# The gate rows and the angle tables of a mixed mLSTM and attention block, given out in 36 small steps

## The chip, the core and the metric

The kernel runs on one core of one Trainium2 chip. Five engines run side by side, each with its own queue of instructions: TensorE (PE) multiplies matrices and transposes, VectorE (DVE), ScalarE (ACT) and GpSimd (POOL) work on elements, and SyncE (SP) starts most of the DMA transfers. PE writes its results to PSUM, which has eight banks here, each of 128 partitions by 512 fp32. The metric is the device time of one execution in microseconds (us), the median over several runs.

## The reference, cut to what matters

One layer is computed for 1024 positions of 1024 numbers, in fp32. A normalized input is projected to twelve segments; two branches follow (an mLSTM over four heads, and differential attention over eight heads), and they are mixed.

```python
proj = jnp.einsum('bsd,de->bse', h, w_in[layer])
(a_q, a_k, a_v, a_o, a_z, a_g, b_q, b_k, b_v, b_z, g_a, g_b) = jnp.split(proj, _split_points(), axis=-1)
qk = jax.nn.silu(centred_depthwise_conv(jnp.concatenate([a_q, a_k], axis=-1), ml_conv_w[layer]))
gates = (a_g.reshape(B, S, 4, ML_HEADS) + ml_gate_b[layer]).transpose(2, 0, 3, 1)
i_fw, lf_fw = gates[0], jax.nn.log_sigmoid(gates[1])
i_bw, lf_bw = gates[2], jax.nn.log_sigmoid(gates[3])
# mlstm: b = cumsum(f); running maximum of i - b; m_t, weights exp(...) and decay per chunk
y_a = hm * jax.nn.sigmoid(a_o) * jax.nn.silu(a_z)
ang = positions[..., None] * inv_freq          # rope: cos(ang), sin(ang) turn b_q and b_k
```

The change touches where the small work is done that depends on `a_g` alone (log-sigmoid, cumulative sums, running maxima, the maximum carried from chunk to chunk, the weights) and on `positions` alone (angles, sines, cosines, two tables). It computes the same numbers.

## The kernel before

**Stages.** The projections come first, then the attention, then the mLSTM, then the mixing. This document is about the second part of the projections, the *pairs' stage*. Numbers are kept as two parts (H and L), so one logical product takes three matmuls.

**Pairs.** `self.pairs` has 16 entries, numbered 0 to 15. Each projects two blocks of 128 columns at once by Strassen's scheme (`pair_units`): seven products, f0 to f6 here, of twelve 128x512 matmuls each (L279), in 14 units of six matmuls. A product writes one PSUM bank under the tag `T`. Its bank is read by ACT (f0, L285), by DVE (f1, f2, f3, L282), and by a *sink* (f3 to f6). I write 8.f3 for product f3 of pair 8.

- Even pairs project columns of `ak` or `aq` and end in `conv_sink`: L344 adds the product to what is saved and writes `cin`, then a convolution with five taps is run in four parts (ACT L358, four times DVE L360, ACT L361, DVE L363, ACT L366, POOL L369). Each part takes a bank `T` of its own. I call these four banks A, B, C and D in their order; each becomes free with its L363.
- Odd pairs project columns of `ao` and `az` and end in `oz_sink` (DVE L318 and L319, ACT L321 and L326), which takes no further bank.

**Weights.** The seven weight forms of a pair are rounded on ACT (L256), and their low parts are made on POOL or DVE (L258), some four products ahead.

**Banks.** Six banks have the tag `T` in this stage (`banks("ps0", T=6)`). A product or a transpose that wants one waits until the last reader of the bank's former content is done.

**The small work.** `ml_gates` returns the products of the gate columns (L667, L668) and three functions. `rows` brings the gates through DRAM into rows of 64 partitions and makes the log-sigmoid, cumulative sums and running maxima; its tiles are named `gch`. `chain` transposes the ends of the chunks (PE L131), carries the maximum over the chunks and `weights` transposes it back and makes four rows of weights. `columns` turns these by nine transposes into columns (`gc_...`, `dec128`). `angle_loads` and `angles` load the positions, transpose them once, reduce the angle (tile `wk`), take sine and cosine on ACT (tile `an`) and copy them to two wide tiles (`rep`). `tables` turns each `rep` by eight transposes, in two banks, into `cosT` and `sinT`, which the next stage reads. `an`, `wk`, both `rep`, and the sinks' `cin`, `y` and `oz` share six buffers of the tag `big`.

**What sets the order.** In this stage PE alone keeps the order in which the program is written (`keep(E.PE)`). DVE, ACT, POOL and SP are put in order by a scheduler, which goes by the written order and by when it believes the operands to be ready. Every engine then works strictly in its order. The written order of the small work is:

```python
more = {1: gl + gmm, 4: [chain], 5: [weights], 6: [columns], 7: [do(self.angle_loads)], 8: [do(self.angles)],
        10: tab[0:2], 11: tab[2:4]}
for i in range(len(self.pairs)):
    w.add(*more.get(i, []), *self.pair_units(i, sinks[i]))
```

So each piece stands as a whole ahead of a pair; `rows` is called with the last gate product, ahead of pair 1.

Of the kernel before, what the change touches and what calls it, by code (L numbers as in the profile page):

```python
# [14 lines left out]
S = 1024  # L15
# [94 lines left out]
class Block:  # L110
# [473 lines left out]
    def angle_loads(self):  # L584
# [6 lines left out]
        posf, self.scol = an[0:8, 672:800], an[:, 808:809]  # L591
# [4 lines left out]
    def angles(self):  # L596


        v, a, an = self.v, self.a, self.an
# [7 lines left out]
        sn, cs = t3(an, 0), t3(an, 1)  # L607
        v.tensor_tensor(out=ang, in0=pos.unsqueeze(2).broadcast_to([128, 8, 32]),
                        in1=self.inv.unsqueeze(1).broadcast_to([128, 8, 32]), op=ALU.mult)
        v.tensor_scalar(out=u, in0=ang, scalar1=1.0 / (2.0 * PI), scalar2=None, op0=ALU.mult)  # L610
        magic = 1.5 * 2.0 ** 23
        v.tensor_scalar(out=nh, in0=u, scalar1=magic * 4096.0, scalar2=None, op0=ALU.add)
        v.tensor_scalar(out=nh, in0=nh, scalar1=-magic * 4096.0, scalar2=None, op0=ALU.add)
        v.tensor_tensor(out=u, in0=u, in1=nh, op=ALU.subtract)
        v.tensor_scalar(out=nl, in0=u, scalar1=magic, scalar2=None, op0=ALU.add)
        v.tensor_scalar(out=nl, in0=nl, scalar1=-magic, scalar2=None, op0=ALU.add)
        for part in two_pi_parts():
            for n in (nh, nl):
                v.scalar_tensor_tensor(out=ang, in0=n, scalar=-part, in1=ang, op0=ALU.mult, op1=ALU.add)
        lim = float(np.nextafter(np.float32(PI), np.float32(0)))  # L620
        v.tensor_scalar(out=ang, in0=ang, scalar1=lim, scalar2=-lim, op0=ALU.min, op1=ALU.max)
        v.tensor_scalar(out=u, in0=ang, scalar1=-1.0, scalar2=None, op0=ALU.mult)
        v.tensor_tensor(out=u, in0=u, in1=ang, op=ALU.max)
# [3 lines left out]
        self.reps = []  # L627
        for src in (cs, sn):
            rep = self.big("rep")[:, 0:S].rearrange("p (k a b) -> p k a b", k=8, a=4)
            v.tensor_copy(rep, src.unsqueeze(2).broadcast_to([128, 8, 4, 32]))  # L630
            self.reps.append(rep)

    def tables(self, i, g):

        if g == 0:
            n = ("cosT", "sinT")[i]
            setattr(self, n, self.tab.tile([128, S], F32, name=n, tag=n))
        dst = getattr(self, ("cosT", "sinT")[i])
        ps = self.bank("T")
        for k in range(4):  # L640
            self.tr(ps[:, k * 128:(k + 1) * 128], self.reps[i][:, 4 * g + k].rearrange("p a b -> p (a b)"))
        self.v.tensor_scalar(out=dst[:, g * 512:(g + 1) * 512], in0=ps, scalar1=self.scol[:, 0:1], scalar2=None, op0=ALU.mult)


    def ml_gates(self):
# [15 lines left out]
        def products(half, part):  # L661
# [9 lines left out]
            if part == 1:  # L671
# [4 lines left out]
                if half == 1:  # L676
                    rows()

        def rows():
            gd = X["gd"]  # L680
# [7 lines left out]
            p.memset(one, 1.0)  # L688
            v.tensor_scalar(out=nx, in0=x, scalar1=-1.0, scalar2=None, op0=ALU.mult)
            v.tensor_tensor(out=nx, in0=nx, in1=x, op=ALU.min)  # L690
            a.activation(out=e, in_=nx, func=AF.Exp)
            v.tensor_scalar(out=u, in0=e, scalar1=1.0, scalar2=None, op0=ALU.add)
# [3 lines left out]
            a.activation(out=iu, in_=ln, func=AF.Exp, scale=-1.0)  # L696
            v.tensor_tensor(out=u, in0=u, in1=iu, op=ALU.mult)
# [4 lines left out]
            for d in range(2):  # L702
                r = slice(32 * d, 32 * d + 32)
                st = slice(None) if d == 0 else slice(None, None, -1)
                v.tensor_tensor_scan(out=b[r, st], data0=one[r, st], data1=lf[r, st], initial=0.0, op0=ALU.mult, op1=ALU.add)
            v.tensor_tensor(out=g, in0=ig, in1=b, op=ALU.subtract)
            for d in range(2):
                r = slice(32 * d, 32 * d + 32)
                st = slice(None) if d == 0 else slice(None, None, -1)
                v.tensor_tensor_scan(out=cm[r, st], data0=g[r, st], data1=g[r, st], initial=-3.0e38, op0=ALU.max, op1=ALU.max)  # L710
            gg = self.dram.tile([2, 4 * NC, L], F32, name="gg")
# [4 lines left out]
            for d in range(2):  # L716
# [3 lines left out]
                v.tensor_copy(ends[r, 1:2], cm[r, c:c + 1])  # L720

        def chain():
# [10 lines left out]
            for i in range(NC - 1):  # L733
                for d in range(2):
                    c, n = (i, i + 1) if d == 0 else (NC - 1 - i, NC - 2 - i)
                    v.tensor_tensor(out=vw(mr, d, n), in0=vw(mr, d, c), in1=vw(er[:, 64:128], d, c), op=ALU.max)
                    v.tensor_tensor(out=vw(mr, d, n), in0=vw(mr, d, n), in1=vw(er[:, 0:64], d, c), op=ALU.add)

        def weights():
# [6 lines left out]
            M, sint, emt, ws, nml, dec = one, u, iu, ln, small(1), small(1)  # L746
            v.tensor_scalar(out=M, in0=cm, scalar1=mst[:, 0:1], scalar2=None, op0=ALU.max)
            a.activation(out=sint, in_=M, func=AF.Exp, scale=-1.0, bias=mst[:, 0:1])
            v.tensor_scalar(out=sint, in0=sint, scalar1=0.5, scalar2=None, op0=ALU.mult)
            v.tensor_tensor(out=b, in0=b, in1=M, op=ALU.add)  # L750
            a.activation(out=emt, in_=b, func=AF.Exp, scale=-1.0)
            v.tensor_tensor(out=nml, in0=ends[:, 1:2], in1=mst, op=ALU.max)
            v.tensor_scalar(out=nml, in0=nml, scalar1=-1.0, scalar2=None, op0=ALU.mult)
            a.activation(out=ws, in_=g, func=AF.Exp, bias=nml[:, 0:1])
            v.tensor_scalar(out=ws, in0=ws, scalar1=1.0 / 32.0, scalar2=None, op0=ALU.mult)
            a.activation(out=dec, in_=mst, func=AF.Exp, bias=nml[:, 0:1])
            v.tensor_scalar(out=M, in0=M, scalar1=-1.0, scalar2=None, op0=ALU.mult)
            X["out"] = dict(negM=M, sint=sint, emt=emt, ws=ws)
            X["dcb"] = dcb = b[:, 0:128]
            v.tensor_copy(dcb, dec.broadcast_to([64, 128]))  # L760

        def columns():
            for nm, src in X["out"].items():
# [7 lines left out]
                self.gc[nm] = dst  # L771
            ps = self.bank("T")
            self.tr(ps[:, 0:64], X["dcb"])
            self.dec = cp.tile([128, 2, 32], F32, name="dec128")
            v.tensor_copy(self.dec.rearrange("p d r -> p (d r)"), ps[:, 0:64])

        mm = [Unit(8 * MM, lambda h=h, i=i: products(h, i), (("ag",),)) for h in range(2) for i in range(2)]
        mm[-1].name = "gates"
        return [Unit(0.0, load)], mm, [Unit(0.2, chain, name="chain", after=(("gates", 17.0),)),
# [823 lines left out]
```

## Time and profile before

| what | value |
|---|---|
| median of 3 runs | 1755.4 us (1752.39 to 1755.79) |
| the profiled execution | 1754.15 us |
| its span, first to last instruction | 1752.4 us |
| PE busy | 1668.2 us, 95% |
| DVE, ACT, POOL busy | 59%, 44%, 34% |
| pairs' stage | pairs 0 to 15: 67.4 to 413.7 us |
| pairs 12, 13, 14, 15, each | 19.04 us |

The profile page gives busy times. Its timeline gives for each group of instructions the start, the duration, and in square brackets the idle time of the engine before it with the instruction that ended the wait. A table by stretches gives busy time of each engine and the granted PE clock (1.00 is full speed) between two times, for all instructions or for those of one tile. Matmuls of one product start 0.23 us apart at full clock, whatever duration is shown for one, because they overlap.

### The profile page before, as it was taken

What the parts mean: (1) busy time and instruction counts of PE and PEld (TensorE: products, weight loads), DVE (VectorE), ACT (ScalarE), POOL (GpSimd) and SP (SyncE); (2) the same over time, 40 slices, a digit from 0 to 9 for tenths busy, and PEclk for the clock granted to TensorE, in tenths of its full rate; (3) what the DMA queues carried; (4) which work ended last, traced back from release to release, by engine and by line L of the source; (5) the groups of instructions that cost most, each with busy time, mean ns of one, the idle gap of its engine ahead of it and who ended that gap; (6) DMA issues with size and microseconds to landing.
All of it is one profiled execution on the core that took longest, in us unless ns stands there. A gap on an engine that the chain in (4) does not pass through costs nothing. (4 is left out here: it accounts for less than half of the span.)

```text
span 1752.4 us, 24818 instructions
## 1 busy us (share of the span) xinstructions
PE 1668.2 (95%) x9119; PEld 1423.2 (81%) x9119; DVE 1037.9 (59%) x1917; ACT 767.4 (44%) x1522; POOL 603.2 (34%) x608
## 2 busy tenths in 40 slices
PE   7998898999999999999999989989999988999998
PEld 6777787788887887898789868889999876878886
DVE  5788788775166666666666655425666733235533
ACT  7444444443245454445545445424655634122211
POOL 4775566664332224323351331222321311222000
PEclk9999999999999999999999999999999999999999
DMA  5343434344633614541625252156454327344222
GB/s 179 92 135 109 133 109 133 108 133 130 147 82 90 148 55 105 132 113 37 168 74 132 64 136 67 63 161 187 138 166 149 97 83 249 119 144 133 84 88 81
DMA packets 190604, 208.15 MB, mean 119 GB/s; under 512 B 12761, under 2 KB 136050, under 8 KB 190482
## 3 DMA queue, kind: packets, MB, share of 16 engines
q1 hardware_dynamic: 189570, 204.98, 40.1%
q8 instruction: 72, 1.18, 0.3%
q10 hardware_dynamic: 912, 1.59, 0.2%
q14 instruction: 50, 0.41, 0.1%
HBM read 143.47 MB, written 63.05 MB: 118 GB/s over the span
## 5 line engine op out<-in xcount | busy, mean ns | idle before, releaser
L416 PE MATMUL pj<-hH,wH 128*128 128x512 f32 x640 | 257.9, 403 | 4.9 <-ACT wH L188 3.1
L416 PE MATMUL pj<-hH,wL 128*128 128x512 f32 x640 | 253.1, 395 | 2.4 <-POOL wL L202 1.8
L416 PE MATMUL pj<-hL,wH 128*128 128x512 f32 x640 | 252.0, 394 | 0.2 <-DVE hL L567 0.2
L882 ACT ACTIVATE e<-S,nm 128x1024 f32<-128x1024 f32 x128 | 143.1, 1118 | 183.0 <-DVE nm L880 182.7
L204 POOL TENSOR_TENSOR wL<-raw,wH 128x1024 fp32r<-128x1024 f32 x41 | 99.7, 2432 | 321.9 <-ACT wH L199 321.9
L903 DVE TENSOR_TENSOR pL<-T,pH 128x512 fp32r<-128x512 f32 x128 | 88.0, 687 | 140.5 <-ACT pH L902 140.5
L880 DVE TENSOR_REDUCE nm<-S 128x1 f32<-128x1024 f32 x128 | 155.8, 1217 | 24.3 <-PE S L878 24.2
L438 PE MATMUL pj<-wH,hH 128*128 128x256 f32 x512 | 147.8, 289 | 0.2
L438 PE MATMUL pj<-wL,hH 128*128 128x256 f32 x512 | 145.2, 284 | 1.4 <-POOL wL L202 1.4
L416 PEld LDWEIGHTS pj<-hH,wL 128*128 128x128 f32 x640 | 121.2, 189 | 30.8 <-POOL wL L202 3.4
L416 PEld LDWEIGHTS pj<-hH,wH 128*128 128x128 f32 x640 | 121.5, 190 | 28.7 <-ACT wH L188 3.5
L438 PE MATMUL pj<-wH,hL 128*128 128x256 f32 x512 | 144.7, 283 | 0.0
L416 PEld LDWEIGHTS pj<-hL,wH 128*128 128x128 f32 x640 | 121.4, 190 | 23.4 <-DVE hL L567 0.6
L416 PE MATMUL pj<-sl_yb,wH 128*128 128x512 f32 x384 | 124.1, 403 | 5.1 <-ACT sl_yb L1287 2.3
L199 ACT CAST wH<-raw 128x1024 fp32r<-128x1024 f32 x56 | 58.8, 1050 | 127.4 <-PE pj L416 112.3
L438 PEld LDWEIGHTS pj<-wL,hH 128*128 128x128 f32 x512 | 97.7, 191 | 2.3 <-POOL wL L202 2.3
L438 PEld LDWEIGHTS pj<-wH,hH 128*128 128x128 f32 x512 | 98.0, 191 | 1.6 <-ACT wH L199 0.6
L438 PEld LDWEIGHTS pj<-wH,hL 128*128 128x128 f32 x512 | 97.8, 191 | 0.9
L878 PE MATMUL S<-kst,qH 128*128 128x512 f32 x256 | 89.9, 431 | 5.7 <-DMA qL<-stk 4.3
L360 DVE SCALAR_TENSOR_TENSOR T<-cin,cols,T 128x512 f32<-128x512 f32 x128 | 89.5, 753 | 8.0 <-ACT T L358 7.1
L416 PEld LDWEIGHTS pj<-sl_yb,wH 128*128 128x128 f32 x384 | 73.3, 191 | 25.3 <-DVE sl_yb L1288 3.3
L889 DVE SCALAR_TENSOR_TENSOR e<-e,r,e 128x1024 f32<-128x1024 f32 x64 | 92.6, 1446 | 1.3
(357 smaller groups left out, 4212.1 us busy)
## 6 DMA issues: line engine op xcount, KB each, us to landing
raw<-in_w_in_dram SPq DMA_DIRECT2D x88, 512.0 KB, 4.1
stk<-hl SPq DMA_DIRECT2D x64, 256.0 KB, 3.6
qH<-stk SPq DMA_DIRECT2D x32, 256.0 KB, 5.5
qL<-stk SPq DMA_DIRECT2D x32, 256.0 KB, 5.6
kst<-stk SPq DMA_DIRECT2D x16, 512.0 KB, 4.4
x<-in_x_dram SPq DMA_DIRECT2D x8, 512.0 KB, 9.8
cak<-y SPq DMA_DIRECT2D x16, 256.0 KB, 4.3
cakH<-cin SPq DMA_DIRECT2D x16, 256.0 KB, 2.0
```

The source lines that it names most:

```text
L199: self.a.copy(wH, raw)
L204: self.p.tensor_tensor(out=wL, in0=raw, in1=wHf, op=ALU.subtract)
L360: v.scalar_tensor_tensor(out=acc, in0=raw[:, o + x:o + x + 512], scalar=w(x), in1=acc, op0=ALU.mult, op1=ALU.add)
L416: self.t.matmul(ps, lhsT=l[:, k, :], rhs=r, start=(n == 0), stop=(n == 23))
L438: self.t.matmul(ps[:, i, :], lhsT=l, rhs=r[:, k, :], start=(kh == 0 and k == 0 and m == 0), stop=(kh == 1 and k == 3 and m == 2))
L878: self.t.matmul(ps[:, o], lhsT=x[:, j, c], rhs=st["k"][:, j, o], start=first, stop=not first)
L880: v.tensor_reduce(out=nm, in_=ps, axis=AX.X, op=ALU.max, negate=True)
L882: a.activation(out=e, in_=ps, func=AF.Exp, bias=nm[:, 0:1], accum_out=Z[:, j, t:t + 1])
L889: v.scalar_tensor_tensor(out=e0, in0=e, scalar=r[:, 0:1], in1=e0, op0=ALU.mult, op1=ALU.add)
L903: v.tensor_tensor(out=pL[:, :, s], in0=ps, in1=pH[:, :, s].bitcast(F32), op=ALU.subtract)
```

## The change

`rows`, `chain`, `weights` and `columns`, and `angle_loads` with `angles` and `tables`, become generators that hand back control after a few instructions. The instructions are the same ones, with three exceptions: `scol` gets a small tile of its own in place of a column of `an`; each of the two copies to `rep` is made in two halves; and the copies of the ends of the chunks come after both running maxima. `rows` still begins with the last gate product (its memsets and four loads); the rest is nine steps. The 36 steps are these nine, 3 of `chain`, 5 of `weights`, and 19 of the angles and tables; `columns` goes in 5 units more. A table of pair, unit and distance gives them places between the units of the pairs.

```diff
     def angles(self, an):
...
+        yield
         v.tensor_tensor(out=ang, in0=pos.unsqueeze(2).broadcast_to([128, 8, 32]), ...)
         v.tensor_scalar(out=u, in0=ang, scalar1=1.0 / (2.0 * PI), scalar2=None, op0=ALU.mult)
+        yield
...
-        self.reps = []
+        reps = []
         for src in (cs, sn):
-            rep = self.big("rep")[:, 0:S].rearrange("p (k a b) -> p k a b", k=8, a=4)
-            v.tensor_copy(rep, src.unsqueeze(2).broadcast_to([128, 8, 4, 32]))
-            self.reps.append(rep)
+            reps.append(self.big("rep")[:, 0:S].rearrange("p (k a b) -> p k a b", k=8, a=4))
+            for k in (0, 4):
+                yield
+                v.tensor_copy(reps[-1][:, k:k + 4], src[:, k:k + 4].unsqueeze(2).broadcast_to([128, 4, 4, 32]))
+        for i in range(2):
+            for g in range(2):
+                yield
+                self.tables(reps[i], i, g)
+        yield
...
             for d in range(2):
+                yield
                 v.tensor_tensor_scan(out=b[r, st], data0=one[r, st], data1=lf[r, st], ...)
+            yield
             v.tensor_tensor(out=g, in0=ig, in1=b, op=ALU.subtract)
             for d in range(2):
+                yield
                 v.tensor_tensor_scan(out=cm[r, st], data0=g[r, st], data1=g[r, st], ...)
...
         def columns():
             for nm, src in X["out"].items():
...
                 self.gc[nm] = dst
+                yield
...
+        of = lambda g, n, cost=0.0: [Unit(cost, lambda: next(g)) for _ in range(n)]
+        return [Unit(0.0, load)], mm, of(X["rows"], 9), of(chain(), 3), of(weights(), 5), of(columns(), 5, 0.2)
...
-            more = {1: gl + gmm, 4: [chain], 5: [weights], 6: [columns], 7: [do(self.angle_loads)], 8: [do(self.angles)],
-                    10: tab[0:2], 11: tab[2:4]}
+            more = {(1, 0): gl + gmm}
+            for (i, k), step, un in (((1, 7), 2, rows[:6]), ((3, 7), 2, rows[6:]), ((5, 5), 2, chain), ((5, 13), 1, ang[:1]),
+                                     ((7, 3), 2, weights), ((8, 3), 1, ang[1:2]), ((8, 8), 1, columns), ((9, 5), 2, ang[2:7]),
+                                     ((11, 5), 2, ang[7:11]), ((13, 5), 2, ang[11:15]), ((15, 4), 2, ang[15:19])):
+                for j, u in enumerate(un):
+                    more.setdefault((i + (k + step * j) // 14, (k + step * j) % 14), []).append(u)
             for i in range(len(self.pairs)):
-                w.add(*more.get(i, []), *self.pair_units(i, sinks[i]))
+                for k, u in enumerate(self.pair_units(i, sinks[i])):
+                    w.add(*more.pop((i, k), []), u)
```

So (8, 8) with distance 1 puts the five steps of `columns` ahead of units 8 to 12 of pair 8, which are both halves of f4, both halves of f5, and the first half of f6.

What the scheduler makes of it is seen in the built programs. First VectorE (DVE) in pair 2. L705 and L710 are the cumulative sums and the running maxima, L706 the row between them, L719, L720 and L731 the copies of the chunks' ends and a memset; L282 and L344 belong to pair 2's products. Before:

```order
L705 SCALAR_TENSOR_TENSOR gch<-gch 32x256 x2
L719 COPY gch<-gch 32x1
L258 TENSOR_TENSOR wL<-raw,wL 128x512
L706 TENSOR_TENSOR gch<-gch 64x256
L719 COPY gch<-gch 32x1
L282 TENSOR_TENSOR u_1281<-T,u_1259 128x512
L710 SCALAR_TENSOR_TENSOR gch<-gch 32x256 x2
L720 COPY gch<-gch 32x1
L731 MEMSET gch 1x64
L720 COPY gch<-gch 32x1
L282 TENSOR_TENSOR u_1259<-T,u_1259 128x512
L344 TENSOR_TENSOR cin<-T,u_1281 128x512
```

And now the same stretch of VectorE's queue, where these lines are L726, L728, L733, L743, L744 and L756:

```order
L726 SCALAR_TENSOR_TENSOR gch<-gch 32x256 x2
L258 TENSOR_TENSOR wL<-raw,wL 128x512
L728 TENSOR_TENSOR gch<-gch 64x256
L282 TENSOR_TENSOR u_1272<-T,u_1250 128x512
L733 SCALAR_TENSOR_TENSOR gch<-gch 32x256 x2
L743 COPY gch<-gch 32x1
L744 COPY gch<-gch 32x1
L743 COPY gch<-gch 32x1
L744 COPY gch<-gch 32x1
L756 MEMSET gch 1x64
L282 TENSOR_TENSOR u_1250<-T,u_1250 128x512
L344 TENSOR_TENSOR cin<-T,u_1272 128x512
```

Though the steps of the running maxima are written into pair 3, they still stand in VectorE's queue ahead of pair 2's L344; only four copies of one column moved.

Second, PE where `columns` stood, ahead of pair 6 (T_1923 is 5.f6, T_1974 is 6.f0, the T between them take the five groups of transposes). Before:

```order
L279 MATMUL T_1923<-TH3_177,wL_1814 128x512
L131 MATMUL T_1942<-ident_146,gch_997 128x64 x2
L131 MATMUL T_1948<-ident_146,gch_997 128x64 x2
L131 MATMUL T_1954<-ident_146,gch_997 128x64 x2
L131 MATMUL T_1960<-ident_146,gch_997 128x64 x2
L131 MATMUL T_1966<-ident_146,gch_996 128x64
L279 MATMUL T_1974<-hH0_170,wH_1836 128x512
```

Now PE does them in pair 8; here the last two groups, with the second half of 8.f5 (T_2417) between them and 8.f6 (T_2473) after them:

```order
L131 MATMUL T_2424<-ident_146,gch_997 128x64 x2
L279 MATMUL T_2417<-hH1_171,wL_2287 128x512
L279 MATMUL T_2417<-hL1_173,wL_2287 128x512
L279 MATMUL T_2417<-hH1_171,wL_2287 128x512 x2
L279 MATMUL T_2417<-hL1_173,wL_2287 128x512
L279 MATMUL T_2417<-hH1_171,wL_2287 128x512
L131 MATMUL T_2466<-ident_146,gch_996 128x64
L279 MATMUL T_2473<-TH3_177,wH_2306 128x512
```

The nine transposes no longer follow each other; each group takes its bank between halves of products, in an even pair.

Third, PE in pair 15, the last pair, where the four groups for the tables now stand, each ahead of a product; shown is the one between 15.f2 (T_3612) and 15.f3 (T_3633) (before, they stood ahead of pairs 10 and 11, two groups each):

```order
L279 MATMUL T_3612<-TL2_180,wL_3458 128x512
L279 MATMUL T_3612<-TH2_176,wL_3458 128x512
L131 MATMUL T_3627<-ident_146,rep_2995 128x128 x4
L279 MATMUL T_3633<-TH0_174,wH_3480 128x512
L279 MATMUL T_3633<-TL0_178,wH_3480 128x512
```

The order of all engines behind this stage is the same in both programs.

More of the change, by code (lines that the diff above doesn't have):

```diff
@@ L594, in angle_loads, with angles @@
         self.v.memset(self.scol[0:64], 0.125)
-    def angles(self):
-        v, a, an = self.v, self.a, self.an
+        yield from self.angles(an)
+    def angles(self, an):
+        v, a = self.v, self.a
+        yield
         ps = self.bank("T")
@@ L676, in products @@
                 if half == 1:
-                    rows()
+                    next(X["rows"])
         def rows():
@@ L771, in columns @@
                 self.gc[nm] = dst
+                yield
             ps = self.bank("T")
```

35 lines of the change are left out of this document (26 added, 9 removed).

## The prediction

> **What bounds the kernel now.** I read the busy times first: PE has 95% of the span, so time is lost only where PE waits or its clock is low. The diff touches the pairs' stage alone, so I next cut that stage by pairs, each from its first matmul to the next pair's. Columns: stretch and length, busy time and count of PE, weight loads, DVE, ACT and POOL, then the granted clock, the DMA share and GB/s.
>
> ```profile
> 115.36:139.88 24.52, 19.46 (x85) 15.54 (x84) 21.29 (x32) 9.77 (x16) 11.81 (x8) 1.00 0.23 66
> 139.88:160.82 20.94, 20.94 (x86) 16.84 (x87) 19.40 (x30) 12.56 (x23) 12.92 (x10) 0.92 0.47 151
> 160.82:182.50 21.68, 19.48 (x88) 15.80 (x86) 17.73 (x35) 7.93 (x14) 13.86 (x16) 1.00 0.34 97
> 182.50:206.63 24.13, 21.93 (x94) 17.62 (x94) 23.53 (x40) 12.83 (x25) 17.04 (x17) 0.93 0.45 156
> 206.63:227.38 20.75, 20.75 (x84) 17.00 (x85) 10.26 (x21) 5.94 (x10) 9.92 (x8) 0.92 0.25 74
> 227.38:246.67 19.29, 19.29 (x87) 15.72 (x85) 18.35 (x29) 10.20 (x18) 12.02 (x10) 1.00 0.50 165
> 246.67:271.85 25.18, 19.64 (x85) 15.64 (x85) 23.29 (x38) 9.38 (x17) 15.47 (x15) 0.95 0.22 62
> 271.85:293.84 21.99, 21.99 (x93) 18.08 (x93) 19.47 (x30) 13.42 (x23) 13.36 (x13) 0.90 0.58 193
> 293.84:316.81 22.97, 20.39 (x96) 16.61 (x94) 16.38 (x26) 8.81 (x16) 15.30 (x14) 1.00 0.33 92
> 316.81:337.57 20.76, 20.76 (x84) 16.98 (x85) 17.25 (x25) 10.57 (x18) 15.05 (x15) 0.92 0.37 126
> 337.57:356.62 19.05, 19.05 (x86) 15.77 (x85) 10.45 (x16) 6.83 (x11) 10.59 (x9) 1.00 0.29 83
> 394.69:413.74 19.05, 19.05 (x86) 15.77 (x85) 17.29 (x27) 11.34 (x20) 11.46 (x9) 1.00 0.31 115
> ```
>
> These are pairs 2 to 12, and 15. An undisturbed pair takes 19.04 (pairs 12 to 15): a product is 19.04/7 = 2.72. Each piece of small work costs twice: as a wait, and as a low clock in the pair behind it (0.92, 0.93, 0.90, 0.92). PE's timeline names the waits, in square brackets, with what ended them:
>
> ```profile
> 139.88 0.77 PE L279 MATMUL T<-hH,wL 128*128 128x512 f32 x1 [4.81 <-DVE cin L344]
> ...
> 182.50 0.50 PE L279 MATMUL T<-hH,wL 128*128 128x512 f32 x1 [2.20 <-DVE y L363]
> ...
> 205.72 0.27 PE L131 MATMUL T<-ident,gch 64*128 64x64 f32 x1 [1.57 <-DVE oz L319]
> ...
> 206.63 0.47 PE L279 MATMUL T<-hH,wH 128*128 128x512 f32 x1 [0.64 <-DVE gc_negM L769]
> ...
> 271.85 0.76 PE L279 MATMUL T<-hH,wL 128*128 128x512 f32 x1 [5.53 <-DVE cin L344]
> ...
> 315.46 0.66 PE L131 MATMUL T<-ident,rep 128*128 128x128 f32 x4 [1.88 <-DVE y L363]
> ...
> 316.81 0.48 PE L279 MATMUL T<-hH,wL 128*128 128x512 f32 x1 [0.70 <-DVE cin L344]
> ```
>
> All are waits for a PSUM bank that DVE still has to read. At 139.88 and 271.85 DVE was late, since rows and angles stood in its queue ahead of L344. At the others transposes took banks out of turn. What DVE did on the tiles `gch` (rows; chain; weights) and `wk` (angles; here only DVE, ACT):
>
> ```profile
> 115.00:139.90 24.90, 0.00 (x0) 0.00 (x0) 12.36 (x18) 1.26 (x3) 0.00 (x0) 0.99 0.23 66
> 162.00:168.10 6.10, 0.00 (x0) 0.00 (x0) 4.19 (x13) 0.00 (x0) 0.00 (x0) 1.00 0.46 129
> 190.00:200.00 10.00, 0.00 (x0) 0.00 (x0) 6.80 (x9) 1.49 (x4) 0.00 (x0) 1.00 0.63 211
> ```
> ```profile
> 250.80:267.50 16.70, 10.05 (x17) 0.84 (x2) 1.00 0.33 94
> ```
>
> The clock behind a wait, for pair 5:
>
> ```profile
> 184.00:187.40 3.40, 3.40 (x10) 2.63 (x9) 3.30 (x6) 2.46 (x5) 2.42 (x3) 0.50 0.32 117
> ```
> ```profile
> 186.52 0.63 PE L279 MATMUL T<-TH,wH 128*128 128x512 f32 x1
> ...
> 189.69 0.39 PE L279 MATMUL T<-TH,wL 128*128 128x512 f32 x1
> ```
>
> The product from 182.50 took 186.52 - 182.50 = 4.02, the next 3.17, instead of 2.72 each: 1.75 lost behind a wait of 2.20. In pairs 6 and 11 some 1.7 went behind two short waits together (1.57 and 0.64; 1.88 and 0.70).
>
> **The change part by part.** What a new place costs, I take from the reads of an undisturbed pair (7) and from transposes already there:
>
> ```profile
> 227.38 0.39 PE L279 MATMUL T<-hH,wL 128*128 128x512 f32 x1
> ```
> ```profile
> 229.12 0.69 DVE L363 SCALAR_TENSOR_TENSOR y<-tz,T 128x512 f32<-128x512 f32 x1
> ...
> 233.16 0.68 DVE L363 SCALAR_TENSOR_TENSOR y<-tz,T 128x512 f32<-128x512 f32 x1
> ...
> 238.30 1.28 DVE L363 SCALAR_TENSOR_TENSOR y<-tz,T 128x512 f32<-128x512 f32 x2
> ```
> ```profile
> 160.30 0.39 PE L279 MATMUL T<-TH,wL 128*128 128x512 f32 x1
> 160.62 0.27 PE L131 MATMUL T<-ident,gch 64*1 64x64 f32 x2
> 160.82 0.50 PE L279 MATMUL T<-hH,wH 128*128 128x512 f32 x1
> ```
> ```profile
> 293.05 1.04 PE L131 MATMUL T<-ident,rep 128*128 128x128 f32 x8
> 293.84 0.48 PE L279 MATMUL T<-hH,wH 128*128 128x512 f32 x1
> ```
>
> Counted from an odd pair's first matmul, the even pair's conv gives back bank A at 229.12 + 0.69 - 227.38 = 2.43, B at 6.46, C at 238.30 + 0.69 - 227.38 = 11.61. Products start at 0, 2.72, 5.44 and so on. A transpose that takes a bank moves each later product one bank on, so some product meets a conv bank before it is free. One or two small transposes cost 160.82 - 160.30 - 0.23 (the step between matmuls) = 0.29; eight wide ones 0.79, so four some 0.45 in a group of their own.
>
> - Rows. By DVE's order the running maxima still stand ahead of pair 2's L344, and 12.36 of DVE's work with them. So the 4.81 stays, and the low clock in pair 3. Gain 0.29, the chain's transposes ahead of pair 4: pair 3 at 20.65.
> - Chain, from pair 4 to 5 and 6. Its 4.19 on DVE is covered by pair 6, where DVE has only 10.26 of work; without that cover it would be paid as a wait, up to 4.19. Pair 4 becomes 19.04. Pair 5: the transposes 0.29, and 5.f4 waits for C, 11.61 - 10.88 - 0.29 = 0.44: 19.77. Pair 6 is clean, 19.04.
> - Weights, from pair 5 to 7 and 8. Their 6.80 lies beside pair 8, which loses the angles. One transpose 0.29; 7.f2 starts at 5.73 and waits for B until 6.46, 0.73: pair 7 at 20.06.
> - Columns, from 5 to 8. Nine transposes in five groups: between 0.79 (all in one piece) and 5 x 0.29 = 1.45; I take 1.3, nearer the small groups. The last takes the bank between B and 8.f6, so that 9.f0 waits for A, 2.43 - 0.29 = 2.14: pair 8 at 22.5. Behind it the low clock, between 0 and 2.1; I take pair 5's 1.75, whose wait of 2.20 is nearest: pair 9, with one transpose of positions, 19.04 + 0.29 + 1.75 = 21.1.
> - Angles, from pair 8 to 9 and 10. DVE's busy time there was 19.47 and 16.38. It gives 2.52 (the copies to `rep`, below) to pairs 11 to 13 and gets 10.05: 43.4 shown. Operations in a row overlap (two L363 in 1.28, one 0.68, so 0.60 apart), about 12%: 38.2 in 21.1 + 19.04 = 40.1. It fits with 2 us to spare. Pair 10, freed of its waits, 19.04; for pair 11 I leave 0.2 for a late read: 19.24.
>
> ```profile
> 265.01 2.52 DVE L630 COPY rep<-an 128x1024 f32<-128x1024 f32 x2
> ```
>
> - Copies to `rep` in halves: four, 2.52 in all, from pair 11 on, where DVE has room (17.25 in pair 11, 10.45 in pair 12); uncovered, 0.6 each.
> - Queues. On SP the load of positions stands behind pair 4's last store instead of pair 6's; the cast for it moves from pair 7 to pair 5 on DVE, where pair 5's other reads are queued behind it until the load has landed, with pair 6's free DVE time as cover. POOL gets nothing. On ACT the sine and the cosine now stand apart and between other functions, with two more table loads of 1.28, beside some 9 us of free ACT time a pair.
> - Tables, from pairs 10 and 11 to 15. Four groups, 4 x 0.45 = 1.8 (0.79 for eight is the lower end, 1.6). 15.f2 would start at 5.89 and waits for B until 6.46, 0.57. 15.f3 would start at 8.16 + 0.9 + 0.57 = 9.63 and waits for C until 11.61, 1.98. Together a gap like those ahead of pairs 6 and 11, so 1.6 of low clock: pair 15 at 19.05 + 1.8 + 0.57 + 1.98 + 1.6 = 25.0.
>
> The sum, pairs 3 to 11 and 15: before 20.94 + 21.68 + 24.13 + 20.75 + 19.29 + 25.18 + 21.99 + 22.97 + 20.76 + 19.05 = 216.74; then 20.65 + 19.04 + 19.77 + 19.04 + 20.06 + 22.5 + 21.1 + 19.04 + 19.24 + 25.0 = 205.44. So 11.3 less: 1754.15 - 11.3 = 1742.9 for the profiled execution. The median, 1755.4, lies 1.2 higher and would give 1744.1; I say 1743.5.
>
> A rule against two of these terms: the Trainium skill, "TensorE: Matmul & The Clock Gate" (Why this matters for your kernels), wants no idle gaps over about 3 us, since the clock halves only after an idle window. By that page the gaps of 2.14 and 0.57 + 1.98 cost no clock. The trace differs: 0.50 behind a gap of 2.20.
>
> **The rivals.**
> - *The angles are still late.* DVE's 2 us to spare go, because the 17 operations on `wk` last longer in the new place than the 10.05 of the old one, or an answer of ACT is late. Past some 2 us more, pair 8's wait of 5.53 and its low clock of 2.1 come back ahead of pair 11: 1743.5 + 7.6 = 1751.1.
> - *The rows' stall goes as well*, 4.81 + 1.9 of clock and a little more: 1736.5. DVE's order speaks against it.
> - *The new bank waits don't appear* (0.44, 0.73, 2.14, 0.57, 1.98 and the clock behind, 3.35): 1743.5 - 9.2 = 1734.3. Against it: they follow from the rotation of banks.
> - *No low clock behind gaps under 3 us*: 1743.5 - 1.75 - 1.6 = 1740.2. Against it, the row of pair 5.
> - *Stalls only change place*, as each piece does DVE's same work: about 1754.
> - *Slower.* ACT stands still at the sine, in order, as it did before:
>
> ```profile
> 255.90 1.28 ACT L625 ACT_TABLE_LOAD   x1
> ...
> 263.41 0.42 ACT L625 ACTIVATE an<-wk 128x256 f32<-128x256 f32 x1 [6.23 <-DVE wk L621]
> ```
>
> Now sine and cosine each have such a place, ahead of the casts (L256) for pair 10. If DVE's half of the angles is more than 4 us late, 10.f4 and a later product wait for their weights, two waits of up to 6.23, and low clocks of 2 behind each: 1743.5 + 12.5 + 4 = 1760.
>
> **How the numbers follow.** Forecast 0.55 (its own range 1740 to 1747.5, the ends of the transposes and clock terms); angles late 0.14; rows' stall gone 0.07; no bank waits 0.06; clock 0.08; only moved 0.07; slower 0.03. The range 1736 to 1752 leaves out no bank waits, moved and slower, 0.16. A run can tell about 0.2%, 3.5 us, from no change: under 1751.9 is faster (0.55 + 0.07 + 0.06 + 0.08, and over half of the late angles: 0.84), 1751.9 to 1758.9 the same (0.12), above it 0.04.
>
> **What would show it.** Right: ahead of pair 3 still some 4.8 with L344; pairs 4, 6, 10 at 19.04; L363 as releaser at 9.f0 (2.1), 15.f2 and 15.f3; pair 15 near 25; DVE's `wk` done before 10.f4's L344. Wrong: an idle PE over 2 us ahead of pair 11; no wait at 9.f0 or in pair 15; pair 3 at 19.04.

## The result, and the profile after

The changed kernel takes 1743.99 us (median of 6; before, on the same chip, 1753.89). The ratio is 0.9935, with a 95% interval of 0.9919 to 0.9951. The prediction was 1743.5. The profiled execution took 1743.21 us, with a span of 1741.4, 11.0 less than before. But its stages show that the 11 us did not come as forecast. Stages are cut at the first matmul of each, in the timeline of PE:

| stretch | before | after | difference |
|---|---|---|---|
| up to the first pair | 67.40 | 67.77 | +0.4 |
| the pairs' stage | 346.34 | 342.72 | -3.6 |
| attention and mLSTM, up to the last stage | 1054.8 | 1053.2 | -1.6 |
| the last stage (mixing) | 283.9 | 277.7 | -6.2 |

The forecast put all 11.3 into the pairs' stage. That stage gave 3.6, and the last stage, whose order of work is the same in both programs, gave 6.2. The table by pairs after the change (columns as before; pairs 2 to 5, 7 to 12 and 15):

```profile
116.19:139.88 23.69, 19.58 (x86) 15.62 (x84) 20.50 (x32) 9.76 (x16) 12.21 (x8) 0.96 0.23 68
139.88:161.59 21.71, 21.71 (x84) 17.49 (x85) 20.27 (x31) 12.50 (x22) 13.74 (x15) 0.89 0.44 146
161.59:181.00 19.41, 19.41 (x85) 15.78 (x84) 12.04 (x18) 6.83 (x11) 12.81 (x10) 1.00 0.27 82
181.00:200.99 19.99, 19.99 (x87) 15.70 (x86) 19.88 (x34) 9.22 (x17) 12.76 (x10) 1.00 0.62 211
...
220.40:240.79 20.39, 19.99 (x87) 15.72 (x85) 20.28 (x30) 10.39 (x19) 13.21 (x10) 1.00 0.46 155
240.79:264.41 23.62, 21.93 (x95) 16.14 (x93) 18.11 (x37) 10.62 (x21) 13.95 (x16) 1.00 0.31 89
264.41:284.30 19.89, 19.89 (x86) 15.93 (x87) 19.51 (x29) 8.00 (x14) 13.42 (x14) 1.00 0.54 186
284.30:307.19 22.89, 20.08 (x85) 15.46 (x84) 18.18 (x30) 14.31 (x22) 12.64 (x10) 1.00 0.24 69
307.19:328.59 21.40, 21.18 (x85) 16.61 (x85) 19.92 (x29) 11.90 (x22) 12.67 (x11) 0.92 0.44 148
328.59:348.00 19.41, 19.41 (x85) 15.78 (x84) 13.24 (x18) 7.11 (x12) 14.79 (x15) 1.00 0.27 82
...
386.83:410.48 23.65, 21.72 (x101) 17.40 (x100) 19.20 (x30) 11.80 (x20) 11.41 (x9) 1.00 0.37 130
```

Two things strike the eye. An undisturbed pair (161.59, 328.59) takes 19.41 where it took 19.04, at full clock and without a wait: something slows the matmuls themselves. And pairs 10 and 11, for which the forecast was 19.04 and 19.24, have lost 3.5 and 2.0 beyond that. PE's waits:

```profile
139.88 0.76 PE L279 MATMUL T<-hH,wL 128*128 128x512 f32 x1 [4.11 <-DVE cin L344]
...
226.83 0.50 PE L279 MATMUL T<-TH,wL 128*128 128x512 f32 x1 [0.40 <-DVE y L363]
...
264.41 0.50 PE L279 MATMUL T<-hH,wL 128*128 128x512 f32 x1 [1.69 <-DVE y L363]
...
299.04 0.47 PE L279 MATMUL T<-hH,wL 128*128 128x512 f32 x1 [0.69 <-ACT wL L256]
...
307.19 0.47 PE L279 MATMUL T<-hH,wL 128*128 128x512 f32 x1 [2.00 <-DVE cin L344]
311.71 0.61 PE L279 MATMUL T<-TH,wH 128*128 128x512 f32 x1 [0.22 <-DVE y L363]
...
393.25 0.50 PE L279 MATMUL T<-TH,wL 128*128 128x512 f32 x1 [0.28 <-DVE y L363]
...
398.40 0.50 PE L279 MATMUL T<-TH,wH 128*128 128x512 f32 x1 [1.65 <-DVE y L363]
```

The waits named in the prediction are there, but for the one at 5.f4: L344 ahead of pair 3 (4.11), B at 7.f2 (226.83), A at 9.f0 (264.41), B and C in pair 15. Those at 299.04 and 307.19, ahead of 10.f5 and of pair 11, are the rival of the late angles.

### The profile page after: what moved, and what is told of

It reads as the page before. It is cut to its first block, busy times and chain, and to the rows that moved or that the text cites. A ratio compares the mean times of both kernels' runs of the same rounds, so it can differ in the third digit from the quotient of the medians.

```text
span 1741.4 us, 24821 instructions
## 1 busy us (share of the span) xinstructions
PE 1663.4 (96%) x9119; PEld 1418.1 (81%) x9119; DVE 1045.8 (60%) x1919; ACT 768.8 (44%) x1524; POOL 601.3 (35%) x608
```

## First experiments: where the matmul became slower, and the last stage faster

In pairs 12 and 14 PE has the same instructions in the same order as before. What differs is SBUF. `scol` got a tile of its own among the constants, and in the built program hH, hL, wH, wL and sl_r all stand 32 bytes higher, while TH, TL and sl_yb stayed. By product, f1, f2, f3 and f6, which stream TH and TL, take 2.80 instead of 2.72 (0.2335 a matmul instead of 0.227). Of those that stream hH and hL, f5 still takes 2.72; f0 and f4 follow a slow product and take 2.74, with only their first five steps above 0.227. In the last stage, matmuls of sl_yb with wH went the other way, from 0.2335 to 0.227. So the first theory: it matters how the streamed operand and the weights stand to each other.

**The kernel before with 32 dead bytes** (a1_before_shift32):

```diff
             self.v.memset(self.mhalf, -0.5)
+            self.cpad = self.const.tile([128, 8], F32, name="cpad")
+            self.v.memset(self.cpad, 0.0)
```

> The kernel before, unchanged but for a 32-byte constant tile that nobody reads, which moves the tiles hH, hL, wH and wL (and sl_r) up by 32 bytes in SBUF, while TH, TL and sl_yb stay. Placement theory (a matmul takes 0.227 us when its weights and its streamed operand start at the same address modulo 64 bytes, and 0.2335 when they differ): pairs 12 to 14 go from 19.04 to 19.41 each, in products f1, f2, f3 and f6 alone; the stage of the pairs gets 5 us longer; in the last stage the matmuls of sl_yb with wH go from 0.2335 to 0.227, some 5 us less; the total stays within 2 us of before. Rival (the 19.41 of the changed kernel comes from its small steps or its order): pairs 12 to 14 stay at 19.04, both stages as before.

Pair 13 and the last stage of this kernel:

```profile
359.46:378.87 19.41, 19.41 (x85) 15.78 (x84) 16.42 (x25) 10.19 (x18) 12.18 (x10) 1.00 0.65 217
1477.00:1752.80 275.80, 264.78 (x1176) 218.27 (x1176) 108.20 (x181) 63.03 (x100) 39.23 (x22) 0.99 0.36 119
```

The last stage of before, for comparison, and of the changed kernel:

```profile
1468.50:1752.40 283.90, 272.54 (x1176) 219.11 (x1176) 108.32 (x181) 62.99 (x100) 39.38 (x22) 0.98 0.35 115
```
```profile
1463.70:1741.40 277.70, 266.19 (x1176) 219.16 (x1176) 108.19 (x181) 62.97 (x100) 39.24 (x22) 0.98 0.34 118
```

With not one step moved, the pair is at 19.41 and the last stage is as short as after the change. Both come from the 32 bytes. The total was to stay within 2 us; it is 1751.84 against 1756.08, ratio 0.998 (0.9966 to 0.9994). Here and below a ratio is to the kernel before, run on the same chip; the chips differ between experiments, so that ratios compare better than times.

**Which distance?** Three kernels moved TH and TL, or hH, hL, wH and wL, by other amounts:

```diff
                 self.TL = [self.tf.tile([128, 4, 512], F32R, name=f"TL{i}") for i in range(4)]
+                self.tpad = self.tf.tile([128, 8], F32, name="tpad")   # a2, a4: 32 bytes; b1: 24, 96 bytes
```
```diff
-        ..., self.const.tile([128, 1], F32, name="scol")
+        ..., self.const.tile([128, 16], F32, name="scol")[:, 0:1]      # a3: 64 bytes
```

> The changed kernel with a 32-byte tile that nobody reads behind TL, which moves TH and TL down by 32 bytes, so that all operands of the pairs' matmuls start alike modulo 64. Placement theory: undisturbed pairs 19.04 instead of 19.41, the last stage as fast as in the changed kernel; 5 us less than it, about 1739. Rival: no change, 1744.

> The changed kernel with scol padded to 64 bytes: hH, hL, wH, wL stand 64 bytes above their place in the kernel before, so alike with TH and TL modulo 64 but not modulo 128. Placement theory with modulus 64: undisturbed pairs 19.04, the last stage's sl_yb matmuls back at 0.2335; total within 1 us of the changed kernel (5 less, 5 more). With modulus 128: pairs stay at 19.41, total about 1749. Rival (order): pairs stay at 19.41, last stage unchanged.

> The changed kernel with a 96-byte tile that nobody reads behind TL: TH and TL now start at 0 modulo 128, as hH, hL, wH, wL and sl_yb do (modulo 256 and 512 they differ). Placement theory in its second form (0.227 us where the two operands start alike modulo 128, 0.2335 where not): pairs 12 to 14 at 19.04, every product 2.72, last stage still fast; 14 times 0.37 = 5 us less than the changed kernel. Modulo 256 or 512: pairs 12 to 14 stay at 19.40. Rival (not the placement): the same, 19.40.

Pair 13 of each, and the last stage of a3 (second row):

```profile
347.52:366.93 19.41, 19.41 (x86) 15.74 (x85) 18.12 (x26) 9.46 (x17) 12.23 (x9) 1.00 0.65 216
```
```profile
347.23:366.63 19.40, 19.40 (x85) 15.74 (x84) 18.13 (x26) 9.15 (x17) 12.22 (x9) 1.00 0.64 216
1462.70:1746.20 283.50, 272.36 (x1176) 219.13 (x1176) 108.54 (x181) 62.94 (x100) 39.43 (x22) 0.98 0.35 115
```
```profile
347.46:366.84 19.38, 19.38 (x86) 15.76 (x84) 18.56 (x27) 10.13 (x18) 12.21 (x9) 1.00 0.65 218
```

All three stayed slow in the pairs: modulo 64 fell with a2 and a3, modulo 128 with b1. In a3 wH is no longer where sl_yb is, and the last stage is back at 283.5. Totals: a2 1740.63 (ratio 0.9924, 0.9906 to 0.9942), a3 1748.53 (0.9963, 0.9952 to 0.9974), b1 1742.85 (0.9923, 0.9903 to 0.9944). The total of a2 lies near the 1739 of a theory that its pairs refute.

**The same with the kernel before** (a4_before_align: the edits of a1 and a2 together).

> The kernel before with both moves (32 bytes ahead, 32 bytes behind TL): all operands alike modulo 64 in both stages. Placement theory: pairs 12 to 14 at 19.04, the last stage 5 us less than before: about 1748.5. Rival: as before, 1754. The difference of this run to the changed kernel with the same placement is then what the small steps alone bring.

Pairs 12 to 14 took 19.40, the last stage 277.1; 1749.95, ratio 0.9973 (0.996 to 0.9985). The theory with 64 was wrong here too. The total came out near the expected one by luck: the pairs' stage grew by only 2.2 (348.49), since the stalls for L344 were shorter than in the kernel before (3.91 and 4.88 instead of 4.81 and 5.53), and the last stage gave 6.8 instead of 5.

**Placement undone, and modulo 256:**

```diff
-        self.nlam = self.const.tile([128, 1], F32, name="nlam")
+        self.nl8 = self.const.tile([128, 8], F32, name="nlam")         # c1: the 32 bytes that nlam takes anyway
+        self.nlam = self.nl8[:, 0:1]
...
-        ..., self.const.tile([128, 1], F32, name="scol")
+        ..., self.nl8[:, 1:2]
```
```diff
+                self.tpad = self.tf.tile([128, 56], F32, name="tpad")  # c2: 224 bytes behind TL
```

> The changed kernel with scol put into the unused rest of nlam's 32 bytes, so that every tile stands at its address of the kernel before; the steps and their order are those of the changed kernel. Placement theory (the new tile's 32 bytes are the cause, by whatever rule of addresses): pairs 12 to 14 at 19.04 instead of 19.41, the stage of the pairs 5 us shorter than in the changed kernel; the last stage 6 us longer, its sl_yb matmuls at 0.2335: total 1744 to 1746. Rival (the steps themselves): pairs stay at 19.41, the last stage stays fast.

> The changed kernel with a 224-byte tile that nobody reads behind TL: TH and TL start at 0 modulo 256 (at 256 modulo 512), hH, hL, wH, wL at 0 modulo 512. Moves by 32 and 96 bytes brought nothing. If the two operands must start alike modulo 256: pairs 12 to 14 at 19.04 and the last stage still fast, 5 us less than the changed kernel. If modulo 512, or if the rule is not one of equal starts: pairs stay at 19.4.

Pair 13 and last stage, c1 first, then c2:

```profile
346.73:365.77 19.04, 19.04 (x85) 15.77 (x84) 18.23 (x26) 9.70 (x18) 11.82 (x9) 1.00 0.66 221
1465.57:1749.30 283.73, 272.05 (x1176) 218.60 (x1176) 108.36 (x181) 62.78 (x100) 39.37 (x22) 0.98 0.35 115
```
```profile
345.70:364.74 19.04, 19.04 (x85) 15.77 (x84) 18.22 (x26) 9.07 (x16) 11.80 (x9) 1.00 0.66 219
1460.07:1737.40 277.33, 266.25 (x1176) 219.21 (x1176) 108.17 (x181) 62.94 (x100) 39.22 (x22) 0.98 0.36 118
```

Both as the placement theory says. By the addresses in the built programs (start modulo 256 of TH and TL, of wH and wL, then the time of one matmul): 224 and 224, 0.227 (before, c1); 224 and 0, 0.2335 (after, a1); 192 and 0 (a2) and 224 and 32 (a3), 0.2333; 128 and 0 (b1), 0.232 to 0.233; 0 and 0 (c2), 0.227. For sl_yb and wH: 0 and 224 (before, c1) and 0 and 32 (a3), 0.2335; 0 and 0, 0.227. In these runs a matmul is fast where both start alike modulo 256, and 3% slower at each of the other distances tried.

The medians were 1744.34 for c1 (0.9934, 0.9913 to 0.9956) and 1740.13 for c2 (0.9913, 0.9887 to 0.9939). The pairs' stage is 340.95 in c1 and 339.81 in c2: with placement as before or mended, it is 1.8 and 2.9 shorter than after, not the 5 us expected. The missing part is in pairs 2 and 10. Pair 2 took 24.73 in c1 and 23.69 in after, because its end waits for DVE's L344, which came at the same time: a faster PE only waits longer there (5.30 in c2, 4.11 in after).

**Placement without the steps** (d2_before_mod256: a1's edit and c2's, on the kernel before).

> The kernel before with a 32-byte constant tile ahead and a 224-byte tile behind TL, both read by nobody: all operands alike modulo 256. Theory: pairs 12 to 14 at 19.04 as before, the last stage 6 us less than before: 1749. The distance from this to the changed kernel with the same placement (1740) is what the steps alone bring, 9 us. Rival (placement is worth nothing by itself): 1755.

1751.47, ratio 0.997 (0.9949 to 0.9991); pairs' stage 345.96, last stage 277.3. Four placements have now been run without and with the steps, so that what the steps alone bring can be read four times. The stages are of one profiled execution each; the totals are the distance of the two ratios, in us, each uncertain by some 4 to 6:

| without, with the steps | pairs' stage | total |
|---|---|---|
| before, c1 | 346.34 - 340.95 = 5.4 | 11.6 |
| a1, after | 350.32 - 342.72 = 7.6 | 7.9 |
| a4, a2 | 348.49 - 342.31 = 6.2 | 8.6 |
| d2, c2 | 345.96 - 339.81 = 6.2 | 10.0 |

So with equal placement the steps are worth 5.4 to 7.6 in the pairs' stage, not 11.3. In the total they are worth more, 8 to 12, and c1, without any change of placement in the matmuls, is by its median as fast as the changed kernel (1744.34). In three of the four, the stretch between the pairs and the last stage, where the order of work is the same, is also 4.5 to 6.3 shorter with the steps; in the fourth it is 2.3 longer, but c1's profiled execution is the slowest of its five. PE's longest wait for a transfer there, near 1040, is 4.9, 3.4, 5.2 and 4.25 us in a1, a4, d2 and before, and 2.66 at most in their four partners. But s2 and d1 below have the steps and wait 4.6 and 4.7, so that it is not shown that the steps bring this part.

## Second experiments: what the steps cost at their new places

Each edit stands on the changed kernel, with its placement.

**One instruction for sine and cosine** (s1_one_sine).

```diff
-        a.activation(out=sn, in_=ang, func=AF.Sin)
-        a.activation(out=cs, in_=u, func=AF.Sin)
+        two = lambda x, st: x[:, 0:1024].rearrange("p (i c) -> p i c", c=256)[:, 0:st + 1:st]
+        a.activation(out=two(an, 1), in_=two(wk, 3), func=AF.Sin)
```

> The changed kernel with sine and cosine taken by one ACT instruction over both halves (512 elements), so that ACT loads its tables twice there and not four times. Theory (ACT's four table loads hold up L326 of pair 9, so that DVE waits for it and reaches L344 of 10.f5 too late): pair 10 falls from 22.9 to about 19.4 and pair 11, without a low clock, from 21.4 to 19.4; 5 us less in all. Rival (DVE is simply full with the 17 operations on wk): the wait of 2.0 ahead of pair 11 stays over 1.5.

In the changed kernel ACT's timeline shows four table loads within 8.3 us, and DVE's the wait that they make (L319 for ACT's `tz`):

```profile
288.52 1.28 ACT L635 ACT_TABLE_LOAD   x1
...
290.89 1.28 ACT L321 ACT_TABLE_LOAD   x1
...
293.31 1.28 ACT L636 ACT_TABLE_LOAD   x1
...
295.55 1.28 ACT L326 ACT_TABLE_LOAD   x1
```
```profile
297.48 0.69 DVE L319 SCALAR_TENSOR_TENSOR T<-tz,T 128x512 f32<-128x512 f32 x1 [2.78 <-ACT tz L326]
```

PE's wait of 0.69 at 10.f5 has the same source: it is for a weight form, whose rounding (L256) stands behind the last of these loads in ACT's queue. With one instruction, DVE's wait is 0.34, and 10.f4 and 10.f5 lose nothing: pair 10 falls from 22.89 to 21.48. But the stall ahead of pair 11 stays, and so does pair 11 (21.26). PE's waits there in s1:

```profile
304.94 0.47 PE L279 MATMUL T<-hH,wL 128*128 128x512 f32 x1 [1.91 <-DVE cin L344]
...
309.45 0.50 PE L279 MATMUL T<-TH,wH 128*128 128x512 f32 x1 [1.53 <-DVE y L363]
```

So the table loads cost 1.4, and the rival holds for the rest: DVE comes late by itself. In the changed kernel the angles' work on `wk` lasts 11.91, not 10.05 (DVE, then ACT):

```profile
276.00:291.60 15.60, 11.91 (x17) 0.42 (x1) 1.00 0.31 113
```

Pairs' stage 340.57, total 1742.97 (0.9926, 0.9899 to 0.9953).

**Other banks for the transposes** (s2_cols_tabs).

```diff
-                ... ((8, 8), 1, columns), ... ((15, 4), 2, ang[15:19])
+                ... ((8, 5), 1, columns), ... ((14, 0), 2, ang[15:19])
```

> The changed kernel with two places changed: the five groups of columns three units earlier in pair 8 (5 to 9 instead of 8 to 12), the four groups for the tables in pair 14 (units 0, 2, 4, 6) instead of pair 15. Theory (what costs is which product meets a conv bank A, B or C): the wait of 1.69 at 9.f0 goes, the transposes stay, pair 8 from 23.6 to 21.7; pair 15 from 23.65 to 19.4, pair 14 from 19.4 to 21.0; 4.5 us less in all. Rival (the transposes themselves, with what they break up between halves of products, are the cost): pair 8 stays over 23, pairs 14 and 15 together stay over 42.

Pairs 8, 14 and 15:

```profile
239.44:261.12 21.68, 21.68 (x94) 16.31 (x93) 15.85 (x34) 9.50 (x18) 13.43 (x15) 1.00 0.26 73
...
364.19:385.02 20.83, 20.83 (x100) 17.06 (x98) 17.86 (x27) 8.21 (x14) 12.26 (x13) 1.00 0.27 76
385.02:404.43 19.41, 19.41 (x85) 15.77 (x84) 17.16 (x27) 11.33 (x20) 11.44 (x9) 1.00 0.33 118
```

As the theory said, and the rival falls: where the transposes come ahead of the conv's banks, no product of pairs 8, 9, 14 and 15 waits for A, B or C, and only the transposes are paid (0.35 of them in pair 13, which takes 19.76). Stage 337.15, total 1739.06 (0.9904, 0.9883 to 0.9926).

**The running maxima held back** (s3_rows_late).

```diff
             yield
+            v.scalar_tensor_tensor(out=ig[:, 0:1], in0=self.lastp1[0:64, 0:1], scalar=0.0, in1=ig[:, 0:1], op0=ALU.mult, op1=ALU.add)
             v.tensor_tensor(out=g, in0=ig, in1=b, op=ALU.subtract)
...
-                ((1, 7), 2, rows[:6]), ((3, 7), 2, rows[6:])
+                ((1, 7), 2, rows[:5]), ((4, 3), 2, rows[5:])
```

`lastp1` is the copy of the latest pair's f0, here pair 4's.

> The changed kernel with the last four steps of rows (the subtraction L728, both running maxima, and the ends) written into pair 4, and held there by a DVE instruction of one column that adds 0 times a number of pair 4's first product. Theory (4.3 us of rows ahead of pair 2's L344 in DVE's queue are what PE waits for ahead of pair 3): the wait of 4.11 falls to under 0.5, pair 2 from 23.7 to about 19.6, pair 3 from 21.7 (or 21.1) to 19.4 without a low clock; 6 us less. Rival (the earlier steps, 7 us in pair 2, are enough to make L344 late): over 2 us of wait stay.

Pairs 2 and 3, and the one wait left there:

```profile
116.08:135.49 19.41, 19.41 (x85) 15.72 (x84) 16.26 (x27) 9.86 (x16) 11.50 (x8) 1.00 0.28 82
135.49:155.93 20.44, 19.65 (x86) 15.71 (x85) 18.90 (x30) 12.38 (x22) 12.55 (x10) 1.00 0.48 155
```
```profile
139.21 0.48 PE L279 MATMUL T<-TH,wH 128*128 128x512 f32 x1 [0.79 <-DVE cin L345]
```

The stall of 4.11 is gone, and 0.79 of it comes back at 3.f1, for 2.f6's read: pair 3 takes 20.44, not the 19.4 that was expected. Stage 337.13, total 1739.23 (0.9907, 0.9882 to 0.9932). The table of the change writes the maxima into pair 3, but DVE took them in pair 2 all the same; a data dependence held them.

**All together** (d1_best: s1, s3, c2, tables as in s2, and these places).

```diff
+                ((5, 11), 1, chain), ... ((7, 11), 1, weights), ... ((10, 2), 1, columns),
+                ((11, 11), 1, ang[2:11]), ((13, 5), 2, ang[11:15]), ((14, 0), 2, ang[15:19])
```

> All of it together, on the changed kernel: the last four steps of rows held to pair 4; chain and weights at unit 11 of pairs 5 and 7, behind the conv's bank C; columns in units 2 to 6 of pair 10; the angles (one instruction for sine and cosine) from unit 11 of pair 11, where DVE has least else to do; tables in pair 14; and TH, TL at 0 modulo 256. Theory: no wait over 0.5 us is left in pairs 2 to 15, undisturbed pairs take 19.04; 14 x 19.04 = 266.6 and for transposes 0.3 + 0.3 + 2.2 + 0.3 + 1.6 = 4.7 and 1 or 2 of low clock behind rows: the stage of the pairs about 321 instead of 342.7, total 1722. Rival (DVE's work only moves, so that other pairs wait): stage over 333, total over 1733.

1733.17, ratio 0.9884 (0.9847 to 0.9921): the fastest of the kernels. The stage took 328.27, 18 less than before, between the theory's 321 and the rival's 333. The clock is full in all of pairs 2 to 15, but five waits of over 0.5 are left. Those of over 1 us:

```profile
135.70 0.47 PE L279 MATMUL T<-hH,wL 128*128 128x512 f32 x1 [1.10 <-DVE cin L345]
...
334.10 0.47 PE L279 MATMUL T<-hH,wL 128*128 128x512 f32 x1 [1.76 <-DVE cin L345]
...
338.78 0.50 PE L279 MATMUL T<-TH,wH 128*128 128x512 f32 x1 [1.69 <-DVE y L364]
```

The angles moved to pairs 11 and 12, and their stall moved with them, now ahead of pair 13. DVE still does its 17 operations on `wk` within some 16 us; whether two halves in two even pairs would hide them was not tried.

## Why the prediction was right in the total and wrong in its terms

The time and the sign were right. The sum behind them was not: it put 11.3 into the pairs' stage, where the steps bring 5.4 to 7.6, and 3.6 with the placement that came along. The rest of the profiled 11.0 came from the last stage (6.2, placement) and from the stretch ahead of it (1.6), to which the prediction gave nothing. That the total was met to 0.5 us is luck. Pair by pair, in us (c2 is the changed kernel without the slow matmuls):

| pair | predicted | after | c2 | what differed |
|---|---|---|---|---|
| 2 | 24.52 | 23.69 | 24.72 | rows' stall stays, as forecast |
| 3 | 20.65 | 21.71 | 20.89 | placement; low clock up to 4.8 into the pair, before 3.2 |
| 4, 6 | 19.04 | 19.41 | 19.04 | only the placement |
| 5 | 19.77 | 19.99 | 19.97 | wait for C at 5.f4 0.33 in c2, not 0.44 |
| 7 | 20.06 | 20.39 | 20.24 | |
| 8 | 22.5 | 23.62 | 23.32 | columns' transposes 2.2, not 1.3 |
| 9 | 21.1 | 19.89 | 19.56 | no low clock behind 9.f0's wait |
| 10 | 19.04 | 22.89 | 23.23 | angles late, ACT's loads |
| 11 | 19.24 | 21.40 | 21.01 | angles late, A's read as well |
| 15 | 25.0 | 23.65 | 23.67 | no low clock; waits as forecast |

- **Rows: right.** "By DVE's order the running maxima still stand ahead of pair 2's L344" gave 4.11 of wait, and s3 removed it by holding back these and the two small steps around them.
- **Banks: right in place and nearly in size.** The idle time in brackets runs from the end shown for the matmul before, 0.39 behind its start, where the step is 0.23; the prediction counts from starts, which is 0.16 more. In c2, where the matmuls are as fast as the prediction took them, idle plus 0.16 is 0.71 at 7.f2, 1.90 at 9.f0, 0.62 and 1.86 in pair 15, and 0.33 at 5.f4, against 0.73, 2.14, 0.57, 1.98 and 0.44. In the changed kernel itself, with its slower matmuls, products come later and wait a little less. s2 shows the mechanism.
- **Angles: the step that failed.** "It fits with 2 us to spare" compared sums of busy time over two pairs. Of the 2 us, 1.2 fell away with the low clock of pair 9, which did not come (21.1 forecast, 19.89 measured). The work on `wk` took 1.9 more than before. And DVE stood 2.78 for ACT, whose extra table loads were costed "beside some 9 us of free ACT time": they stood in ACT's order ahead of an answer that DVE needed. The rival of the late angles (0.14) had mechanism and place right; it came in at 3.9 and 2.2 beyond the forecast of pairs 10 and 11 (6.0, of which 0.7 is placement), against its price of 7.6. The wait at 10.f5 is, in small, what the slowest rival (0.03) described.

  Why the same 17 operations took longer can be read from DVE's and POOL's timelines side by side. After the change, seven of them ran beside an instruction of POOL and took 0.78 to 1.47 each; the other ten took 0.28 to 0.43. Before, four ran beside POOL for most of their time and took 1.27 to 1.41, the rest 0.28 to 0.43. One operation before, and the same one after with the POOL instruction beside it:

```profile
255.32 0.43 DVE L614 TENSOR_TENSOR wk<-wk 128x256 f32<-128x256 f32 x1
```
```profile
281.70 1.29 POOL L235 TENSOR_TENSOR s3f<-raw 128x512 f32<-128x512 f32 x1
281.81 1.47 DVE L621 TENSOR_TENSOR wk<-wk 128x256 f32<-128x256 f32 x1
```

  "POOL gets nothing" is true of the change, but the work on weights that POOL has anyway counted. That it makes the operations longer is read from their coincidence; no run moved POOL's work to test it.
- **Columns: mis-sized.** A group of two transposes cost 0.47, where the prediction had at most 0.29. PE's timeline in pair 8, with the group between the halves of 8.f4:

```profile
253.55 0.40 PE L279 MATMUL T<-hH,wH 128*128 128x512 f32 x1
253.88 0.34 PE L131 MATMUL T<-ident,gch 64*128 64x64 f32 x2
254.15 0.50 PE L279 MATMUL T<-hH,wH 128*128 128x512 f32 x1
254.48 0.40 PE L279 MATMUL T<-hL,wH 128*128 128x512 f32 x1
```

  From matmul to matmul it is 0.60, 0.37 more than the step; with the next matmul, 0.33 behind, 0.47. The place is not the reason, for the group ahead of the whole of 8.f4 cost as much (matmuls at 251.70, 252.29 and 252.63). The 0.29 was read from transposes of another shape (64*1 in their row, here 64*128), and it left out the slow step behind them: the matmul after 160.82 starts at 161.16, another 0.11. Five groups made 2.2. The wide groups in pair 15 cost some 0.45 each, as forecast.
- **Low clock: two terms fell, 1.75 and 1.6.** It did not come behind the waits of 1.69 and 0.28 + 1.65. The records of the granted clock in the traces show what decides it. In each trace, all stretches of low clock start on one grid of 3.41 us, and each lasts for whole steps of the grid at 0.50, but for one cut off by the end of the span. In pairs 1 to 15 of all fourteen traces, a step at full clock with 1.86 us or more of idle PE was followed by a low step (33 of 33), and one with 1.76 or less by a full step. (In the rest of the kernel the border is less sharp: steps with 1.16 to 1.93 idle are found on both sides.) So it matters how much of a wait falls into one step. Here are two waits of 2.00 ahead of pair 11, in steps of the grid, the changed kernel first, then s2 (PE's busy time is the first number behind the comma, the granted clock the third from the right):

```profile
305.15:308.56 3.41, 1.41 (x7) 1.18 (x7) 3.38 (x5) 0.88 (x2) 2.54 (x3) 1.00 0.02 5
308.56:311.97 3.41, 3.19 (x9) 1.98 (x8) 3.40 (x6) 1.39 (x3) 0.45 (x1) 0.50 0.56 154
```
```profile
299.62:303.03 3.41, 2.16 (x10) 1.41 (x8) 2.47 (x5) 1.24 (x2) 3.33 (x3) 1.00 0.11 33
303.03:306.45 3.42, 2.67 (x12) 2.17 (x12) 3.42 (x6) 1.98 (x2) 2.92 (x3) 1.00 0.08 12
```

  In the first, all 2.00 of idle time (3.41 - 1.41) fall into one step, and the next is at 0.50. In the second they are split into 1.25 and 0.75; the step from 306.45 is at 1.00. Of the eight kernels with a wait of 1.91 to 2.03 there, four had the low clock and four had not. The wait of 1.69 was too short for any place on the grid, and the two in pair 15 stand 5.15 apart, so that no step holds both.

  The rule that the prediction set against these terms (the Trainium skill, "TensorE: Matmul & The Clock Gate", Why this matters for your kernels: no idle gaps over about 3 us) would have given them right. It doesn't hold as it stands, for waits of 2.00 and, in c1 ahead of 10.f5, of 1.86 were followed by a low clock. The Trainium skill, under the same title (Part 1: The HAM clock gate), says that the window which is watched runs free, so that the same wait may fall differently into it. The traces agree: their grid has steps of 3.41 us and stands differently to the work in each run.
- **Low clock was also priced twice.** Behind a late L344 the next product waits for A, since DVE is late there too. 11.f1 starts 4.52 behind 11.f0 in the changed kernel (clock 0.70 and a wait of 0.22) and 4.51 in s1, where PE waits 1.53 at the next product instead. Where DVE sets the time, the low clock costs nothing.
- **Pairs 3 to 9 and 15 together** were forecast at 167.16 and took 168.07 in after and 165.73 in c2; what the sum missed in this stage lies in pairs 10 and 11.

## What to carry to other kernels

Work that is spread over many small steps is hidden only if each engine's queue puts it behind what others wait for. A scheduler that goes by readiness may pull it forward; here it took a data dependence, not a place in the written order, to hold it. Where a transpose takes a bank decides which product meets a bank that is freed late, so count the banks from the last slow reader and put the transposes ahead of it. And compare an untouched stretch of the profile before believing a total: in the profiled executions the last stage, where not one instruction had moved, gave more than the stage that was changed.

## What was not expected of the hardware

- The placement: 32 bytes of SBUF make a matmul of 128x512 fp32 take 0.2335 instead of 0.227, and in these runs the two operands' starts modulo 256 tell which. It is worth 0.37 a pair and 6 us in the last stage. Why it is so, the runs do not show.
- The low clock follows PE's idle time per step of a grid of 3.41 us, not the length of a wait: in the pairs' stage from 1.86 us on, and not at 1.76 or less.
- The stretch between the pairs and the last stage, with the same order in all of the kernels, took 1051.6 (s3) to 1059.3 (a1) in the profiled executions. One such difference is a transfer that comes late; in d1 PE waits for it as follows, while in the changed kernel its longest wait for a transfer there is 2.66. That is why the argument above goes by stages, and why a total of one execution says little.

```profile
1017.97 0.79 PE L914 MATMUL S<-kst,qH 128*128 128x512 f32 x1 [4.74 <-DMA qL<-stk]
```
